# RG-LRU's second half in RWKV's buffers, and RWKV's sample steps in LRU's stream

## The chip, the core and the metric

The kernel runs on one core of a Trainium2 chip. The metric is the device time of one execution in microseconds; before the change it was 1579.41 us, the median of three runs (1573.84 to 1581.77). One further execution was taken with the profiler; it took 1583.56 us, and the trace quoted here is of that one.

## The reference, cut to what matters

One layer of a hybrid recurrent decoder, for a prompt of 1024 tokens from a zero state and for 8 sample sequences of one token each that continue from given states. The normalised input of width 1024 goes through one projection of 3456 columns, whose output feeds three groups of heads side by side:

```
pr, ph, pl = split(xn @ w_in)                       # RWKV, HGRN, LRU columns
# A) RWKV-7, 6 heads of 64, token by token
S = S * w_t + (S @ -kk_t) outer (kk_t * a_t) + v_t outer k_t ;  out_t = S @ r_t
o_r = (groupnorm(out) + sum(r * k * r_k) * v) * g
# B) HGRN2, 6 heads of 64
S = f_t * S + (1 - f_t) outer i_t ;  o_t = S^T q_t ;  o_h = rmsnorm(o) * g_norm * silu(gate)
# C) RG-LRU, 256 channels
xc = conv4(xb) ;  r = sigmoid(xc @ wa + ba) ;  i = sigmoid(xc @ wx + bx)
h_t = a_t * h_{t-1} + sqrt(1 - a_t^2) * i_t * xc_t ;  o_l = h * gelu(gate)
x = x + concat(o_r, o_h, o_l) @ w_out
x = x + relu(rmsnorm(x) @ w1)^2 @ w2 ;  y = rmsnorm(x)
```

The new states of all three groups are outputs as well. For the 8 sample sequences the recurrences are one step each.

## The kernel before, in words

**The phases.** All data is float32. A weight column of 128 is split into a high part `wh` and a low part `wl`, the activations into `xh` and `xl`, and each dense product is three matmuls per row tile of 128 (`wh` with `xh`, `wh` with `xl`, `wl` with `xh`; `dense_steps`). The mixed phase (the first half of the span) makes the input projections column by column (`in<column>_<half>_<start>`, 48 matmuls a column in the second half, in two chunks of 256 and 264 tokens), and beside them runs the recurrences, whose matmuls are small. Then come the output projection (`out`), the norm and the MLP (`up`, `dn`). Tokens 0 to 511 are half 0; tokens 512 to 1023 and the 8 sample tokens are half 1 (520 columns). The projections come in the order `ORDER`: in half 1 `w0 r0 h0 r1 r2 h1 h2 l0 l1`, so LRU's two tiles are last. Its `l0` is columns 2944 (`xb`) and 3200 (`gl`), `l1` is 3072 and 3328; the last HGRN column ahead of them is 2816.

**What sets the order.** The order of TensorE's instructions is written by a planner, `weave`, while the program is built. It holds seven streams (generators) and a filler, the dense work. A step of a stream ends by yielding a number, an estimate of how long the other engines need before the next step, or an event that it waits for. `weave` keeps a model clock `now`; at each turn it takes a stream that is due, and the filler if none is. The other engines' instructions are placed by the framework's scheduler, by readiness and priority. The streams are RWKV's chain (`rw_chain`), two of its inverse (`rw_inverse`), its operands (`rw_operands`), its finish (`rw_finish`), HGRN (`hgrn`), and LRU (`lru`). RWKV works in twelve parts (three pairs of heads `j`, two halves, two quarters of 256 tokens), HGRN in six (`j` and half), LRU in four (tile `t` and half). In names of tiles the numbers are `j` or `t`, then half, then quarter.

**Buffers that gate the projections.** A projected column of HGRN or LRU is kept in one of eight `hpm` buffers (520 + 3 wide) in SBUF, one of RWKV in one of six `pm` buffers (520 wide). A projection takes its buffer with `take`, which waits for the planner's count `free`. HGRN takes four (`f`, `q`, `i`, `g`) and gives them back at the end of `hg_run`, that is after the part's own sample step (`hg_sample`: `hsrow`, `hso`, `hsq`); RWKV takes three and gives them back when the operands of the second quarter are made; LRU takes two, `xb` and `gl`, and gives them back at its end. LRU's gelu scratch `lq` and its convolved input `lxc` have one buffer each, shared by the two tiles of a half. The output projection uses `pm` buffers too, without `take`: the residual `xr` (a transfer from `xt`) and the squares `sq`.

**LRU's tail.** `lru` makes the gelu of `gl` (L1156 to L1159), convolves `xb` into `lxc` (L1165 to L1170), makes two gates with block-diagonal matmuls (`lg`), a square root and a scan on the Vector engine (L1202), and multiplies by the gelu (L1206).

**RWKV's sample steps.** `rw_sample_lora` makes the three low-rank terms of the sample tokens (`s_lora`), and `rw_sample(j)` the one step of the pair `j`: `s_kk` (a norm), `rows_sa` and `rows_v` (the state's row sums, whose second operand is a diagonal product of `v`, made by GpSimd), `rso` (the output), `s_mean` and `s_var` (group norm). Each is one or two matmuls with Vector's work before and after it. They stand in HGRN's stream: `rw_sample(j)` runs before `hg_run(j, 1)`. Their state `s_st`, scratch `s_tm` and diagonal product `s_dg` take HGRN's own scratch buffers (tags `kh`, `qe`, `kt`).

**PSUM.** Five kinds of banks: `big` (2, dense products), `ra` (2, RWKV's inverse), `ch` (1, the chain), `h` (2, HGRN and the samples), and `o` (1). A user of `o` asks for it with `bank_o`, which waits in the planner's model until `L_O` = 1.6 us after the last use (`used_o`); on the chip a user waits for the reader of the use before.

**Weights.** Each column's weight comes by one transfer of SP's queue into `raw`; the Scalar engine makes `wh` and minus `wh` in `wl`, and a transfer that GpSimd issues adds the weight into `wl`. There are two buffers each of `wh` and `wl`, one of `raw`.

Of the kernel before, what the change touches and what calls it, by code (L numbers as in the profile page):

```python
# [17 lines left out]
P = 128  # L18
# [3 lines left out]
NB = 8  # L22
# [30 lines left out]
def kernel(ctx: ExitStack, tc: tile.TileContext, i, o):  # L53
# [397 lines left out]

    def shifted(hf, col, name, out, tag, bufs):

        k = col // P
        pr = rwp.tile([P, HT + 16], F32, tag="praw", name=f"praw_{name}", bufs=1)
        pm = rwp.tile([P, HW], F32, tag=tag, name=f"pm_{name}", bufs=bufs)

        def evac(pt, c0, n):
            take_out(hf, pr[:, c0:c0 + n], pt)

        yield from in_proj(hf, col, evac, shift=True)
        mu = vec("mu", k)
        n = HT if hf == 0 else HW
        G.tensor_scalar(pm[:, :n], pr[:, :n], omm[:, k:k + 1], 0.0, op0=ALU.mult, op1=ALU.add)
        V.scalar_tensor_tensor(pm[:, 1:HT], pr[:, 0:HT - 1], mu, pm[:, 1:HT], op0=ALU.mult, op1=ALU.add)
        if hf == 0:
            G.tensor_copy(bnd[:, k:k + 1], pr[:, HT - 1:HT])
        else:
            V.scalar_tensor_tensor(pm[:, 0:1], bnd[:, k:k + 1], mu, pm[:, 0:1], op0=ALU.mult, op1=ALU.add)
            V.scalar_tensor_tensor(pm[:, HT:HW], pr[:, HW:HW + NB], mu, pm[:, HT:HW], op0=ALU.mult, op1=ALU.add)  # L470
        out.append(pm)
# [320 lines left out]
    def rw_sample_lora():  # L792
        tcol = slice(HT, HW)
        xwa, sg = lora[1]
        out = hgp.tile([P, 3, 3, NB], F32, name="s_lora")
        for q, (w, x) in enumerate(((wup, xwa), (aup, xwa), (gup, sg))):
            pl = ps("h", f"s_lora{q}")
            for j in range(3):
                mm(pl[:, j * NB:(j + 1) * NB], w[:, j * P:(j + 1) * P], x[:, tcol])
            V.tensor_copy(out[:, q], pl[:, 0:24].rearrange("p (j b) -> p j b", b=NB))  # L800
        return out

    def rw_sample(j, lora):
# [11 lines left out]
        st = hgp.tile(B3, F32, tag="kh", name=f"s_st{j}", bufs=1)  # L815
        tm = hgp.tile(B3, F32, tag="qe", name=f"s_tm{j}", bufs=1)
        dg = hgp.tile(B3, F32, tag="kt", name=f"s_dg{j}", bufs=1)
# [11 lines left out]
        G.tensor_tensor(dg, bc(id64[:, None, :], B3), bc(v[:, :, None], B3), op=ALU.mult)  # L829
        yield D21  # L830
        pn = ps("h", f"s_kk{j}")
        mm(pn[:, 0:NB], bones, q)
        V.tensor_scalar(q, pn[:, 0:NB], 1e-24, None, op0=ALU.max)
# [11 lines left out]
        def sums(x, name):  # L845

            pd = ps("h", f"rows_{name}{j}")
            mm(pd, bones, x.rearrange("p b v -> p (b v)"))
            return pd.rearrange("p (b v) -> p b v", v=64)
# [4 lines left out]
        pd = sums(tm, "sa")  # L854
        V.tensor_tensor(tm, pd, cols(ka), op=ALU.mult)
        V.tensor_tensor(st, st, tm, op=ALU.add)
        yield D24
        pd = sums(dg, "v")
# [4 lines left out]
        po = ps("h", f"rso{j}")  # L863
        for b in range(NB):
            for h in range(2):
                hp = slice(h * 64, h * 64 + 64)
                mm(po[hp, b:b + 1], st[hp, b, :], r[hp, b:b + 1])
        V.tensor_copy(os_, po[:, 0:NB])
        yield D26
        pn = ps("h", f"s_mean{j}")  # L870
        mm(pn[:, 0:NB], bones, os_)
        V.scalar_tensor_tensor(os_, pn[:, 0:NB], -1.0 / 64.0, os_, op0=ALU.mult, op1=ALU.add)
        V.tensor_tensor(q, os_, os_, op=ALU.mult)
# [9 lines left out]
        V.tensor_tensor(mix[j][:, T:TS], os_, g, op=ALU.mult)  # L883

# [244 lines left out]
    def lru_proj(t, hf):  # L1129
# [3 lines left out]
        for w in ("xb", "gl"):  # L1133
            yield from take("hpm")
            x.append(hp_tile(f"l{w}{t}_{hf}"))
        xb, gl = x
# [7 lines left out]
    def lru(t, hf):  # L1144
        yield ("lru", t, hf)
        xb, gl = lruin[t, hf]
        gq = hgp.tile([P, HW], F32, tag="lq", name=f"lq{t}_{hf}", bufs=1)
# [59 lines left out]
        free["hpm"] += 2  # L1207
# [17 lines left out]
    def mixed(k, hf):  # L1225

        if k < 3:
            return [("P", 6 * hf + 2 * k + 1)] + [("HG", k, 1)] * hf
        return [("HG", k - 3, hf) if k < 6 else ("LRU", k - 6, hf)]

    def out_proj(hf):
# [12 lines left out]
        def evac(m, c0, cn, pt, xt):  # L1244
# [3 lines left out]
            if m == 0:  # L1248
                act(a, xm, AF.Square)
            else:  # L1250
                sq = rwp.tile([P, HW], F32, tag="pm", name=f"sq{m}_{c0}", bufs=RPM)
                act(sq[:, :cn], xm, AF.Square)
                V.tensor_tensor(a, a, sq[:, :cn], op=ALU.add)
# [3 lines left out]
        def load(m):  # L1257
            ws[m] = next_w(m + 1 < lead or m >= lead)
            xts[m] = rwp.tile([P, HW], F32, tag="pm", name=f"xr{m}_{hf}", bufs=RPM)
# [99 lines left out]
    def hgrn():  # L1359
# [3 lines left out]
        for hf in range(2):  # L1363
            if hf == 1:
                yield ("lora", 1)
                s_lora = rw_sample_lora()
            for j in range(3):
                if hf == 1:
                    yield from rw_sample(j, s_lora)
                yield from hg_run(j, hf)  # L1370

# [56 lines left out]
    def norms():  # L1428
        yield from norm2(*CH[0], lambda nm: rwp.tile([P, HW], F32, tag="pm", name=nm, bufs=RPM))
# [3 lines left out]
    with tc.manual_schedule(engines={mybir.EngineType.PE}):  # L1433
# [3 lines left out]
               each(lru, *((t, hf) for hf in range(2) for t in range(2)))], dense_work)  # L1437
# [166 lines left out]
```

## Time and profile before

| | |
|---|---|
| time, median of three runs | 1579.41 us (1573.84 to 1581.77) |
| profiled execution | 1583.56 us |
| its span | 1581.8 us |
| granted TensorE clock, mean | 0.972 |
| TensorE matmul busy | 1500.9 us, 95% of the span |
| TensorE weight load | 84% |
| Vector, Scalar, GpSimd | 48%, 42%, 24% |

The profile names the engines PE (TensorE matmul), PEld (its weight load, which overlaps), DVE (Vector), ACT (Scalar), POOL (GpSimd) and SP (which issues transfers). The span is the time from the first to the last instruction in the trace. The clock row of the page gives, for 40 equal slices of 39.5 us, the clock that TensorE was granted, in tenths (9 is 90% or more). A row of the timeline has start, duration in us, engine, line, operation and tiles (out<-in), shapes, a count, and in brackets the idle time ahead of it with what ended it. A row of the waits has the waiting engine's instruction, what released it, total us, times and the longest.

### The profile page before, as it was taken

What the parts mean: (1) busy time and instruction counts of PE and PEld (TensorE: products, weight loads), DVE (VectorE), ACT (ScalarE), POOL (GpSimd) and SP (SyncE); (2) the same over time, 40 slices, a digit from 0 to 9 for tenths busy, and PEclk for the clock granted to TensorE, in tenths of its full rate; (3) what the DMA queues carried; (4) which work ended last, traced back from release to release, by engine and by line L of the source; (5) the groups of instructions that cost most, each with busy time, mean ns of one, the idle gap of its engine ahead of it and who ended that gap; (6) DMA issues with size and microseconds to landing.
All of it is one profiled execution on the core that took longest, in us unless ns stands there. A gap on an engine that the chain in (4) does not pass through costs nothing.

```text
span 1581.8 us, 31488 instructions
## 1 busy us (share of the span) xinstructions
PE 1500.9 (95%) x13112; PEld 1322.7 (84%) x13112; DVE 757.3 (48%) x1799; ACT 665.3 (42%) x1433; POOL 382.5 (24%) x531
## 2 busy tenths in 40 slices
PE   8989999999998899978999999999999999999997
PEld 6767777888898888866798899889898989988887
DVE  7777866756566665574555222222222222222224
ACT  4544656546544556255434324232332323233232
POOL 4553323224335324323312110101111010101011
PEclk9989999998999999799999999999999999999999
DMA  4334334344434334235442544535344454544242
GB/s 152 125 68 96 84 81 94 79 83 98 91 75 96 74 81 91 62 73 124 119 128 81 107 80 99 102 83 104 83 104 83 102 92 85 102 86 101 47 93 108
DMA packets 53086, 146.98 MB, mean 93 GB/s; under 512 B 6960, under 2 KB 7248, under 8 KB 52944
## 3 DMA queue, kind: packets, MB, share of 16 engines
q0 software_dynamic: 22976, 65.33, 24.9%
q1 hardware_dynamic: 29824, 79.61, 16.1%
q8 instruction: 103, 1.69, 0.5%
q14 instruction: 39, 0.32, 0.1%
q10 hardware_dynamic: 144, 0.04, 0.0%
HBM read 138.87 MB, written 6.07 MB: 92 GB/s over the span
## 4 chain that ended last, share of the span: by engine, by line
PE 72%; DVE 10%; issue 6%; ACT 5%; DMA 4%; POOL 2%; POOLq 0%; SPq 0%; DVEq 0%; ACTq 0%
PE up L76 22%; PE dn L76 19%; PE in L76 13%; PE out L76 4%; PE ch L76 2%; PE W L76 2%; PE Y L76 2%; PE sc L76 1%; PE gram L76 1%; DMA wl_out<-in_w_out 1%; DVE rq L1035 1%; PE ho L76 1%; DMA raw_in<-in_w_in 1%; DMA wl_w<-in_w 1%; ACT gsq L768 1%
## 5 line engine op out<-in xcount | busy, mean ns | idle before, releaser
L76 PE MATMUL in<-xl,wh_in 128*128 128x512 f32 (+3 forms) x648 | 223.4, 345 | 2.1 <-DVE xl L385 2.1
L76 PE MATMUL in<-xh,wh_in 128*128 128x512 f32 (+3 forms) x648 | 223.9, 345 | 0.0
L76 PE MATMUL dn<-hh,wl_w 128*128 128x264 f32 (+2 forms) x696 | 223.2, 321 | 0.3 <-DMA wl_w<-in_w 0.2
L76 PE MATMUL dn<-hh,wh_w 128*128 128x264 f32 (+2 forms) x696 | 222.8, 320 | 0.0
L76 PE MATMUL dn<-hl,wh_w 128*128 128x264 f32 (+2 forms) x696 | 222.7, 320 | 0.0
L76 PE MATMUL in<-xh,wl_in 128*128 128x512 f32 (+3 forms) x648 | 221.4, 342 | 0.5 <-DVE wl_in L293 0.3
L1492 DVE TENSOR_TENSOR mix<-mix,dn 128x512 f32<-128x512 f32 (+2 forms) x192 | 98.4, 512 | 243.4 <-PE dn L76 243.4
L296 POOL DMA_DIRECT2D wl_w<-in_w x86 | 75.2, 877 | 575.4 <-ACT hh L1422 305.9
L291 ACT ACTIVATE wh_w<-raw_w 128x512 fp32r<-128x512 f32 (+1 forms) x90 | 70.7, 785 | 281.6 <-PE dn L76 228.0
L1421 DVE SCALAR_TENSOR_TENSOR rl<-up,rl 128x512 f32<-128x512 f32 (+2 forms) x96 | 49.5, 516 | 204.5 <-ACT rl L1420 204.4
L76 PE MATMUL up<-nxh,wh_w 128*128 128x264 f32 (+1 forms) x512 | 145.9, 285 | 0.1
L76 PE MATMUL up<-nxl,wh_w 128*128 128x264 f32 (+1 forms) x512 | 145.0, 283 | 0.5 <-POOL nxl L1318 0.5
L76 PE MATMUL up<-nxh,wl_w 128*128 128x264 f32 (+1 forms) x512 | 145.3, 284 | 0.0
L76 PEld LDWEIGHTS dn<-hh,wl_w 128*128 128x128 f32 x696 | 130.8, 188 | 14.1 <-DMA wl_w<-in_w 4.4
L76 PEld LDWEIGHTS dn<-hl,wh_w 128*128 128x128 f32 x696 | 130.9, 188 | 10.1
L76 PEld LDWEIGHTS dn<-hh,wh_w 128*128 128x128 f32 x696 | 131.0, 188 | 9.3
L76 PEld LDWEIGHTS in<-xl,wh_in 128*128 128x128 f32 x648 | 127.4, 197 | 13.4 <-DVE xl L385 4.2
L76 PEld LDWEIGHTS in<-xh,wl_in 128*128 128x128 f32 x648 | 127.1, 196 | 11.1 <-issue 1.0
L76 PEld LDWEIGHTS in<-xh,wh_in 128*128 128x128 f32 x648 | 127.3, 196 | 10.6 <-issue 0.7
L1420 ACT ACTIVATE rl<-up 128x512 f32<-128x512 f32 (+2 forms) x96 | 43.3, 451 | 141.0 <-PE up L76 140.9
L76 PE MATMUL up<-nl,wh_w 128*128 128x512 f32 x256 | 101.5, 397 | 0.0
L76 PE MATMUL up<-nh,wl_w 128*128 128x512 f32 x256 | 101.5, 396 | 0.0
(461 smaller groups left out, 3328.3 us busy)
## 6 DMA issues: line engine op xcount, KB each, us to landing
raw_in<-in_w_in SPq DMA_DIRECT2D x53, 512.0 KB, 3.4
wl_in<-in_w_in POOLq DMA_DIRECT2D x43, 512.0 KB, 5.7
raw_w<-in_w SPq DMA_DIRECT2D x32, 512.0 KB, 3.5
raw_w<-in_w SPq DMA_DIRECT2D x64, 256.0 KB, 2.7
wl_w<-in_w POOLq DMA_DIRECT2D x58, 256.0 KB, 4.1
wl_w<-in_w POOLq DMA_DIRECT2D x28, 512.0 KB, 5.6
raw_out<-in_w_out SPq DMA_DIRECT2D x16, 512.0 KB, 3.5
out_y_prompt<-yt SPq DMA_DIRECT2D x16, 256.0 KB, 2.0
```

The costliest lines, as they stand in the source:

```text
L76: PE.matmul(out, lhsT, rhs, start=start, stop=stop)
L291: act(wh[:, ks], raw[:, ks], AF.Copy)
L296: G.dma_start(wl[:, ks], src[:, ks], accum_op=ALU.add)
L768: act(sq, raw[:, g * 64:(g + 1) * 64], AF.Square, bias=sums[:, 0, g:g + 1], accum_out=sums[:, 1, g:g + 1])
L1035: V.tensor_tensor(qp[g][hp, h, :], qef[hp, gc], q[hp, gc], op=ALU.mult)
L1420: act(rl[:, :n], pt[:, :n], AF.Relu)
L1421: V.scalar_tensor_tensor(rl[:, :n], pt[:, :n], 0.0, rl[:, :n], op0=ALU.max, op1=ALU.mult)
L1492: V.tensor_tensor(x2[m][:, c0:c0 + n], x2[m][:, c0:c0 + n], pt[:, :n], op=ALU.add)
```

## The change

Three things are edited.

1. LRU's projections and its gelu scratch. `lru_proj` takes three buffers (`xb`, `gl`, `gq`) instead of two: in half 0 three `hpm`, in half 1 three `pm`. The scratch `gq` was the shared `lq` buffer. All `pm` buffers become 523 wide instead of 520 (`pm_tile`). `lru` gives three back.
2. RWKV's sample steps move from HGRN's stream to LRU's: after LRU's half 0 come the low-rank terms, the three sample steps, and then LRU's half 1. The output projection waits for an event of each sample step (`RS`) instead of the end of HGRN's part.
3. The sample steps' buffers. Their matmuls write the one bank `o` through `bank_o` instead of the two banks `h`. The state `s_st` takes LRU's `xc` buffer, the scratch `s_tm` the `lq` buffer that LRU has left. The diagonal product has no buffer of its own any more: it is written into `s_tm` after the state update that reads it.

```diff
+    def pm_tile(name):
+        return rwp.tile([P, HW + 3], F32, tag="pm", name=name, bufs=RPM)
...
     def rw_sample_lora():
...
-            pl = ps("h", f"s_lora{q}")
+            pl = yield from bank_o(f"s_lora{q}")
             for j in range(3):
                 mm(pl[:, j * NB:(j + 1) * NB], w[:, j * P:(j + 1) * P], x[:, tcol])
+            used_o()
...
     def rw_sample(j, lora):
...
-        st = hgp.tile(B3, F32, tag="kh", name=f"s_st{j}", bufs=1)
-        tm = hgp.tile(B3, F32, tag="qe", name=f"s_tm{j}", bufs=1)
-        dg = hgp.tile(B3, F32, tag="kt", name=f"s_dg{j}", bufs=1)
+        st = hgp.tile([P, HW], F32, tag="xc", name=f"s_st{j}", bufs=1)[:, 0:NB * 64].rearrange("p (b v) -> p b v", v=64)
+        tm = hgp.tile(B3, F32, tag="lq", name=f"s_tm{j}", bufs=1)
...
-        G.tensor_tensor(dg, bc(id64[:, None, :], B3), bc(v[:, :, None], B3), op=ALU.mult)
         yield D21
-        pn = ps("h", f"s_kk{j}")
+        pn = yield from bank_o(f"s_kk{j}")
         mm(pn[:, 0:NB], bones, q)
+        used_o()
...
         V.tensor_tensor(st, st, tm, op=ALU.add)
+        G.tensor_tensor(tm, bc(id64[:, None, :], B3), bc(v[:, :, None], B3), op=ALU.mult)
         yield D24
-        pd = sums(dg, "v")
+        pd = yield from sums(tm, "v")
...
-        pn = ps("h", f"s_var{j}")
+        pn = yield from bank_o(f"s_var{j}")
         mm(pn[:, 0:NB], bones, q)
         mm(pn[:, NB:2 * NB], bones, bo)
+        used_o(5.0)
...
+        ev(("RS", j), 1.5)
...
     def lru_proj(t, hf):
...
-        for w in ("xb", "gl"):
-            yield from take("hpm")
-            x.append(hp_tile(f"l{w}{t}_{hf}"))
-        xb, gl = x
+        for w in ("xb", "gl", "gq"):
+            yield from take("pm" if hf else "hpm")
+            x.append((pm_tile if hf else hp_tile)(f"l{w}{t}_{hf}"))
+        xb, gl, gq = x
...
     def lru(t, hf):
...
-        xb, gl = lruin[t, hf]
-        gq = hgp.tile([P, HW], F32, tag="lq", name=f"lq{t}_{hf}", bufs=1)
+        xb, gl, gq = lruin[t, hf]
...
-        free["hpm"] += 2
+        free["pm" if hf else "hpm"] += 3
...
     def mixed(k, hf):
         if k < 3:
-            return [("P", 6 * hf + 2 * k + 1)] + [("HG", k, 1)] * hf
+            return [("P", 6 * hf + 2 * k + 1)] + [("RS", k)] * hf
...
     def hgrn():
...
         for hf in range(2):
-            if hf == 1:
-                yield ("lora", 1)
-                s_lora = rw_sample_lora()
             for j in range(3):
-                if hf == 1:
-                    yield from rw_sample(j, s_lora)
                 yield from hg_run(j, hf)
+
+    def lru_and_samples():
+        for t in range(2):
+            yield from lru(t, 0)
+        yield ("lora", 1)
+        s_lora = yield from rw_sample_lora()
+        for j in range(3):
+            yield from rw_sample(j, s_lora)
+        for t in range(2):
+            yield from lru(t, 1)
...
-               each(lru, *((t, hf) for hf in range(2) for t in range(2)))], dense_work)
+               lru_and_samples()], dense_work)
```

The order of TensorE is the same in both programs up to the place where `s_lora` now stands, and again from the second half's output projection on. Between these the planner writes another order; three places follow. The rows are line, operation, tiles (out<-in, with a serial number at each name's end), shape, and a count.

**TensorE where column 2944 begins (the first column of LRU's half 1).** Before, between the last product of column 2816 and the first of 2944, with the rest of that stretch left out at the dots (`W`, `Y` are RWKV's inverse, `ch` its chain, `oT` and `gate` its finish; `ho`, `hoT` HGRN's output, `hsrow`, `hso`, `hsq` HGRN's sample step of part 1):

```order
L76 MATMUL in2816_1_256_7845<-xh7_3302,wl_in2816_1_7577 128x264
...
L76 MATMUL W3_2_1_1_8067<-xm_2_1_1_7737,sa_2_1_1_7735 64x64 x8
L81 MATMUL hoT_1_1_8096<-ident_79,hot_1_1_8012 128x128 x4
L76 MATMUL Y3_2_1_1_8102<-ym_2_1_1_7736,wm3_2_1_1_8066 64x64 x8
...
L76 MATMUL hsrow1_8139<-hsdg1_8122,bones_84 128x512
...
L81 MATMUL oT_1_1_1_8157<-ident_79,ot_1_1_1_8077 128x128 x4
...
L76 MATMUL gate_1_1_1_8170<-pm_xg1_3608,gup_162 128x256
L76 MATMUL hso1_8173<-hq1_1_6529,hsst1_8120 64x1 x16
L76 MATMUL W5_2_1_1_8194<-xm_2_1_1_7737,sa_2_1_1_7735 32x32 x8
L76 MATMUL hsq1_8205<-hssq1_8191,bones_84 128x8
L76 MATMUL in2944_1_0_8242<-xh0_3295,wh_in2944_1_7797 128x256
```

And after the change:

```order
L76 MATMUL in2816_1_256_8007<-xh7_3302,wl_in2816_1_7650 128x264
L76 MATMUL in2944_1_0_8077<-xh0_3295,wh_in2944_1_7829 128x256
...
L76 MATMUL Y1_2_1_1_8082<-ym_2_1_1_7893,wm1_2_1_1_8028 64x64 x8
L76 MATMUL ch_1_1_1_7635<-st2_1_1_1_8021,az_186 128x64
L76 MATMUL in2944_1_0_8077<-xl1_3304,wh_in2944_1_7829 128x256
...
L76 MATMUL in2944_1_0_8077<-xh7_3302,wh_in2944_1_7829 128x256
L76 MATMUL W2_2_1_1_8123<-xm_2_1_1_7894,sa_2_1_1_7892 64x64 x8
...
L76 MATMUL hsrow1_8142<-hsdg1_8096,bones_84 128x512
L76 MATMUL ch_1_1_1_7635<-mv_1_1_1_6737,bt_1_1_1_6492 128x64
```

Column 2944 now follows 2816 at once, and the work that stood between them stands inside it and behind it.

**Vector in LRU's half 1, from the scan of tile 0 on.** Before (L1202 is tile 0's scan, L1206 its last product; L1156 to L1159 are the gelu of tile 1, L1165 to L1170 its convolution, which tile 1's gate matmul reads):

```order
L1202 SCALAR_TENSOR_TENSOR lxc0_1_8460<-lxb0_1_8232,lcar_202,lq0_1_8454 128x512
...
L1206 SCALAR_TENSOR_TENSOR mix6_75<-lgl0_1_8233,lxc0_1_8460 128x520
...
L1156 TENSOR_SCALAR lq1_1_8844<-lq1_1_8844 128x520
L1165 TENSOR_SCALAR lxc1_1_8850<-lxb1_1_8428,vt_77 128x520
L1157 TENSOR_TENSOR lq1_1_8844<-lq1_1_8844,lgl1_1_8429 128x520
L1168 SCALAR_TENSOR_TENSOR lxc1_1_8850<-lxb1_1_8428,vt_77,lxc1_1_8850 128x512
...
L1159 SCALAR_TENSOR_TENSOR lgl1_1_8429<-lq1_1_8844,lgl1_1_8429 128x520
```

After (the lines are shifted by nine: L1211 is the scan, L1215 the last product, L1165 to L1168 the gelu, L1174 to L1179 the convolution; L1069 are the state updates of HGRN's part 2):

```order
L1165 TENSOR_SCALAR lgq1_1_8506<-lgq1_1_8506 128x520
L1166 TENSOR_TENSOR lgq1_1_8506<-lgq1_1_8506,lgl1_1_8505 128x520
...
L1211 SCALAR_TENSOR_TENSOR lxc0_1_8539<-lxb0_1_8066,lcar_202,lgq0_1_8068 128x512
...
L1168 SCALAR_TENSOR_TENSOR lgl1_1_8505<-lgq1_1_8506,lgl1_1_8505 128x520
...
L1069 SCALAR_TENSOR_TENSOR hst0_2_1_9009<-hst7_2_0_4183,wl_2_1_8910,ad_2_1_9006 128x64
L1215 SCALAR_TENSOR_TENSOR mix6_75<-lgl0_1_8067,lxc0_1_8539 128x520
...
L1174 TENSOR_SCALAR lxc1_1_8886<-lxb1_1_8504,vt_77 128x520
...
L1177 SCALAR_TENSOR_TENSOR lxc1_1_8886<-lxb1_1_8504,vt_77,lxc1_1_8886 128x512
```

The gelu of tile 1 now stands around the scan of tile 0 instead of behind its end, and state updates of HGRN's part 2 stand ahead of the convolution and among its steps.

**TensorE's users of bank `o` around the sample step of pair 1.** After the change, with everything that uses other banks left out at the dots (`pw` to `bt` are the operands of RWKV's part of pair 1, half 1, first quarter):

```order
L76 MATMUL pw_1_1_0_5714<-pm_wa1_3338,wup_158 128x256
...
L76 MATMUL s_kk1_5797<-s_q1_5729,bones_84 128x8
...
L76 MATMUL pc_kk1_1_0_5826<-bones_84,t2_1_1_0_5710 128x2 x2
...
L76 MATMUL rows_sa1_5872<-s_tm1_5719,bones_84 128x512
...
L81 MATMUL pb_kk1_1_0_5898<-ident_79,t4_1_1_0_5712 128x128 x2
...
L76 MATMUL pa_1_1_0_5949<-pm_wa1_3338,aup_159 128x256
...
L76 MATMUL rows_v1_5969<-s_tm1_5719,bones_84 128x512
...
L81 MATMUL vT_1_1_0_6010<-ident_79,bt_1_1_0_5983 128x128 x4
...
L76 MATMUL rso1_6065<-sm_r_176,s_st1_5718 64x1 x16
...
L76 MATMUL s_mean1_6103<-s_os1_5733,bones_84 128x8
...
L76 MATMUL s_var1_6141<-s_q1_5729,bones_84 128x8
...
L81 MATMUL bt_1_1_0_6228<-ident_79,kz_185 128x128 x4
```

Before, these operands stood together, the sample step came behind them, and it wrote the `h` banks:

```order
L76 MATMUL pw_1_1_0_5717<-pm_wa1_3338,wup_158 128x256
...
L76 MATMUL pc_kk1_1_0_5740<-bones_84,t2_1_1_0_5713 128x2 x2
...
L81 MATMUL pb_kk1_1_0_5822<-ident_79,t4_1_1_0_5715 128x128 x2
...
L76 MATMUL pa_1_1_0_5873<-pm_wa1_3338,aup_159 128x256
...
L81 MATMUL vT_1_1_0_5931<-ident_79,bt_1_1_0_5924 128x128 x4
...
L76 MATMUL bonus_1_1_0_6104<-t2_1_1_0_5713,bones_84 128x256
...
L76 MATMUL s_kk1_6235<-s_q1_6197,bones_84 128x8
...
L76 MATMUL rows_sa1_6325<-s_tm1_6186,bones_84 128x512
...
L76 MATMUL s_var1_6501<-s_q1_6197,bones_84 128x8
```

The six uses of the sample step now alternate with those of the operands in the one bank.

More of the change, by code (lines that the diff above doesn't have):

```diff
@@ L455, in shifted @@
         pr = rwp.tile([P, HT + 16], F32, tag="praw", name=f"praw_{name}", bufs=1)
-        pm = rwp.tile([P, HW], F32, tag=tag, name=f"pm_{name}", bufs=bufs)
+        pm = pm_tile(f"pm_{name}") if tag == "pm" else rwp.tile([P, HW], F32, tag=tag, name=f"pm_{name}", bufs=bufs)
         def evac(pt, c0, n):
@@ L845, in sums @@
         def sums(x, name):
-            pd = ps("h", f"rows_{name}{j}")
+            pd = yield from bank_o(f"rows_{name}{j}")
             mm(pd, bones, x.rearrange("p b v -> p (b v)"))
+            used_o()
             return pd.rearrange("p (b v) -> p b v", v=64)
@@ L853, in rw_sample @@
         yield D23
-        pd = sums(tm, "sa")
+        pd = yield from sums(tm, "sa")
         V.tensor_tensor(tm, pd, cols(ka), op=ALU.mult)
         V.tensor_tensor(st, st, tm, op=ALU.add)
+        G.tensor_tensor(tm, bc(id64[:, None, :], B3), bc(v[:, :, None], B3), op=ALU.mult)
         yield D24
-        pd = sums(dg, "v")
+        pd = yield from sums(tm, "v")
         V.tensor_tensor(tm, pd, cols(kn), op=ALU.mult)
@@ L862, in rw_sample @@
         yield D25
-        po = ps("h", f"rso{j}")
+        po = yield from bank_o(f"rso{j}")
         for b in range(NB):
@@ L867, in rw_sample @@
                 mm(po[hp, b:b + 1], st[hp, b, :], r[hp, b:b + 1])
+        used_o()
         V.tensor_copy(os_, po[:, 0:NB])
         yield D26
-        pn = ps("h", f"s_mean{j}")
+        pn = yield from bank_o(f"s_mean{j}")
         mm(pn[:, 0:NB], bones, os_)
+        used_o()
         V.scalar_tensor_tensor(os_, pn[:, 0:NB], -1.0 / 64.0, os_, op0=ALU.mult, op1=ALU.add)
@@ L1250, in evac @@
             else:
-                sq = rwp.tile([P, HW], F32, tag="pm", name=f"sq{m}_{c0}", bufs=RPM)
+                sq = pm_tile(f"sq{m}_{c0}")
                 act(sq[:, :cn], xm, AF.Square)
@@ L1258, in load @@
             ws[m] = next_w(m + 1 < lead or m >= lead)
-            xts[m] = rwp.tile([P, HW], F32, tag="pm", name=f"xr{m}_{hf}", bufs=RPM)
+            xts[m] = pm_tile(f"xr{m}_{hf}")
             nc.gpsimd.dma_start(xts[m][:, :n], i["xt"][m * P:(m + 1) * P, s0:s0 + n])
@@ L1428, in norms @@
     def norms():
-        yield from norm2(*CH[0], lambda nm: rwp.tile([P, HW], F32, tag="pm", name=nm, bufs=RPM))
+        yield from norm2(*CH[0], pm_tile)
         for c in CH[1:]:
```

## The prediction

> **What bounds the kernel now.** I read the page first (part 1, then the slices), then busy time by stage, then TensorE's row-by-row timeline where a stage loses time, and last the list of who waited for whom.
>
> ```profile
> span 1581.8 us, 31488 instructions
> PE 1500.9 (95%) x13112; PEld 1322.7 (84%) x13112; DVE 757.3 (48%) x1799; ACT 665.3 (42%) x1433; POOL 382.5 (24%) x531
> PEclk9989999998999999799999999999999999999999
> ```
>
> TensorE is busy 95% of the span, so time can come only from its idle stretches and from the stretches at a low clock. The lowest slice of the clock row (a 7) lies about 633 to 672 us, inside the second half of the mixed phase, which the change rearranges. Busy time in five stretches around it (columns: stretch, its length, busy us and count of PE, PEld, DVE, ACT, POOL, granted clock, DMA share, GB/s):
>
> ```profile
> 580.00:621.60 41.60, 40.41 (x669) 37.09 (x668) 25.11 (x69) 25.68 (x64) 13.51 (x21) 1.00 0.36 78
> 621.60:632.17 10.57, 7.46 (x176) 6.57 (x172) 5.58 (x19) 7.71 (x40) 6.22 (x9) 1.00 0.59 135
> 632.17:643.20 11.03, 9.77 (x94) 7.53 (x95) 5.13 (x16) 0.65 (x3) 4.65 (x7) 0.50 0.06 25
> 643.20:652.65 9.45, 9.45 (x57) 9.16 (x58) 4.23 (x15) 0.61 (x2) 4.67 (x5) 0.50 0.10 29
> 652.65:662.00 9.35, 9.08 (x65) 7.92 (x65) 6.22 (x17) 2.66 (x4) 1.70 (x4) 1.00 0.49 103
> ```
>
> Up to 621.6 PE is nearly full at clock 1.00. Then 3.1 us idle, then 20.5 us at clock 0.50. The timeline of PE there:
>
> ```profile
> 602.71 0.43 PE L76 MATMUL ch<-st,az 128*128 128x64 f32 x2
> 603.15 0.28 PE L76 MATMUL in<-xh,wl_in 128*128 128x256 f32 x1
> 603.27 0.28 PE L76 MATMUL in<-xh,wh_in 128*128 128x264 f32 x1
> ...
> 629.54 0.63 PE L81 MATMUL hoT<-ident,hot 128*128 128x128 f32 x4 [1.65 <-DVE gs L765]
> 630.10 0.68 PE L76 MATMUL Y<-ym,wm 64*64 64x64 f32 x16
> 632.58 1.12 PE L76 MATMUL W<-xm,sa 64*64 64x64 f32 x16 [1.43 <-DVE rh L724]
> 633.63 2.07 PE L76 MATMUL hsrow<-hsdg,bones 128*128 128x512 f32 x2
> 639.28 1.19 PE L76 MATMUL gate<-pm_xg,gup 128*128 128x256 f32 x2 [0.84 <-DVE mix L782]
> 643.58 0.41 PE L76 MATMUL in<-xl,wh_in 128*128 128x256 f32 x1
> 643.80 0.41 PE L76 MATMUL in<-xh,wl_in 128*128 128x256 f32 x1
> ```
>
> Dense products (`in`) follow each other every 0.12 us at 603; between 621.6 and 643.2 there is none, only the small matmuls of the recurrences, each waiting for another engine; after it they come every 0.22 us. I call this the hole. Its cause stands in the code, not in a row: LRU's half-1 projections take two `hpm` slots, all eight are held by HGRN's parts 1 and 2 of that half, and part 1 gives its four back only after its sample step (`hsq` of part 1 is the last matmul before `in` resumes).
>
> Who waited for whom on PE from 340 to 830 us (total, times, longest):
>
> ```profile
> PE lg L76 <- DVE lxc L1168: 6.0, 1, 6.0
> PE out L76 <- DMA wl_out<-in_w_out: 3.1, 2, 2.0
> PE gate L76 <- DVE mix L782: 2.5, 3, 1.0
> PE pb_kk L81 <- DVE s_bo L839: 2.3, 1, 2.3
> PE ho L76 <- DVE hst L1060: 1.8, 3, 0.9
> PE s_var L76 <- DVE s_q L873: 1.4, 1, 1.4
> PE ho L76 <- ACT ad L1051: 1.1, 1, 1.1
> PE bonus L76 <- ACT kt L544: 0.4, 1, 0.4
> ```
>
> Apart from the hole, the largest wait is LRU's last gate matmul, 6.0 us at 711.
>
> **The change, part by part.** *(a) LRU half 1 in RWKV's slots.* The projections of LRU's second half now take `pm` slots, which RWKV's operands release before HGRN's part 1 ends. In the new PE order the dense work of column 2944 begins right behind column 2816, and `hsrow`, `hso`, `hsq` of part 1 stand inside it. What was in the hole is still done, beside dense work. Idle time recovered: (10.57 - 7.46) + (11.03 - 9.77) = 4.4 us. The clock: 9.77 + 9.45 = 19.2 us were busy at 0.50. Two shapes tell what full clock gives. One is the dense spacing, 0.22 against 0.12 (45% less). The other is `W`, 1.12 at half clock, of which the timeline has just ahead, still at 1.00:
>
> ```profile
> 627.22 0.68 PE L76 MATMUL W<-xm,sa 64*64 64x64 f32 x14
> ```
>
> That is 0.68 for 14 of its 16 (39% less). I take 40%: 7.7 us. Together 12.1 us. Bounds: 4.4 (the clock falls elsewhere instead) to 4.4 + 9.6 = 14.0 (everything at half clock scales by two). I stay near the upper end because both shapes were measured and the small work gets dense neighbours.
>
> The Trainium skill ("TensorE: Matmul & The Clock Gate", Terms) prices a throttled stretch at its length times one minus the clock share: 20.5 x 0.5 = 10.2 us, an estimate, which would make the sum below 2.5 us better. The same page (Part 1) has the full clock return after about 3.4 us of sustained work; the row 643.20:652.65 shows 9.45 us of gapless matmuls still at 0.50, so the trace agrees on the half clock and not on how soon it ends.
>
> *(b) The tail of LRU.* `gq`, the gelu scratch, no longer shares one buffer between LRU's tiles 0 and 1. Vector's rows ahead of the 6.0 us wait:
>
> ```profile
> 706.57 0.42 DVE L1156 TENSOR_SCALAR lq<-lq 128x520 f32<-128x520 f32 x1
> 707.36 0.69 DVE L1157 TENSOR_TENSOR lq<-lq,lgl 128x520 f32<-128x520 f32 x1
> 709.67 0.69 DVE L1159 SCALAR_TENSOR_TENSOR lgl<-lq,lgl 128x520 f32<-128x520 f32 x1
> 735.06 1.57 DVE L1060 SCALAR_TENSOR_TENSOR hst<-hst,wl,ad 128x64 f32<-128x64 f32 x5
> ```
>
> The first two move into tile 0's square-root wait: -1.1. The state updates `hst` of HGRN part 2 move ahead of that gate matmul, six of them at 1.57 / 5: +1.9, and in return `ho`, now behind the gate matmul, finds them done: -1.8 - 1.1. The buffer `xc` is still shared, so the 6.0 us wait itself stays. Sum -2.1; bounds -4.0 (no `hst` cost) to +6.0 (the same wait once more).
>
> *(c) Samples on bank `o`.* 21 uses (3 for the lora, 6 for each of three samples) leave the two `h` banks for the single `o` bank, where each use must wait for the reader of the one before. For RWKV's own uses of `o` the waits for a reader are `gate` 2.5 and `bonus` 0.4, 2.9 us on some 70 uses (10 in each of six half-1 parts, 8 of LRU, a few left from half 0): 0.04 each. 21 x 0.04 = +0.9. Bounds: 0 to 21 x 1.0 = +21 (the longest one each time); I take the mean, since the kernel's planner spaces these uses as it does the others.
>
> *(d) Samples earlier.* They keep their instructions: per sample the state load, the store, and the same Vector, Scalar and GpSimd operations; the diagonal product moves into `tm` behind the state update. Their waits (`pb_kk` behind `s_bo` 2.3, `s_var` 1.4) are rearranged, not removed: 0, bounds -3.7 (both vanish) to +3.7 (both twice). Behind a waiting `s_var` on PE stand RWKV's chain and the dense products.
>
> *(e) The queues.* The transfers that are moved past (count, KB, us to landing), GpSimd's issues of such adds (x86: 75.2 us, 877 ns each), and, for (f), the two casts that make a weight's buffers:
>
> ```profile
> xr<-in_xt POOLq DMA_DIRECT2D x8, 256.0 KB, 3.8
> wl_in<-in_w_in POOLq DMA_DIRECT2D x23, 512.0 KB, 5.7
> L296 POOL DMA_DIRECT2D wl_w<-in_w x86 | 75.2, 877 | 575.4 <-ACT hh L1422 305.9
> 712.91 1.06 ACT L291 ACTIVATE wh_out<-raw_out 128x1024 fp32r<-128x1024 f32 x1
> 714.00 1.06 ACT L295 ACTIVATE wl_out<-wh_out 128x1024 fp32r<-128x1024 f32 x1
> ```
>
> The two loads of `xr` now stand later on POOL, since their slots are LRU's: `xr0` takes a free slot, `xr1` waits for LRU tile 0's scan. Behind `xr1` stand the chain's `ws` and then the weight adds of `out3`; the `ws` needs a state that PE produces next to the gate matmul that waits for the same tile 0. So 0; bounds 0 to +3.8, one `xr` landing. SP's order of weight loads does not move against the dense products.
>
> *(f) Weights.* Without the hole a buffer freed by one column must be refilled while the next is multiplied: 2 x 1.06 + 0.88 + 5.7 = 8.7 us. The thinnest column is 3072 (48 products at 0.12, one `Y` 0.68, three `ch` 0.43, one `gram` of 32 small matmuls taken as a `Y`: 8.4): +0.3, bounds 0 to +2.
>
> Sum: -12.1 - 2.1 + 0.9 + 0 + 0 + 0.3 = -13.0 us. The profiled execution took 1583.6 us (span 1581.8, 1.8 around it), so 1570.6 for it; it is 4.2 above the median of the runs, 1579.4. On the median: 1566.4, and I say 1567.
>
> **The rivals.** *The clock goes elsewhere.* The new order has two stretches almost without dense work: state product, chain end, `W` and `gram` of column 128, and `hS`, `sc`, `ho`, `Y` in column 2816. If each loses the clock as the hole did, (a) keeps only its idle part: -13.0 + 7.7 = -5.3, 1574. For it: the trace's hole. Against it stands a like stretch of the same half:
>
> ```profile
> 414.00:421.60 7.60, 7.00 (x127) 6.50 (x125) 3.31 (x11) 5.53 (x24) 1.62 (x3) 1.00 0.64 139
> ```
>
> It kept its clock, so the waits inside the hole matter, not the small matmuls alone.
>
> *The hole stays*, with another keeper: 2944's weights or its `pm` slots come late. For it: only POOL's order, where these weights stand behind the chain's `ws`. Against it: the columns before are filled with small work. Time 1579.
>
> *More than the hole*: both sample waits (3.7) and half of the gate wait (3) go as well: -13.0 - 6.7, 1560.
>
> *Slower: bank `o` becomes the serial resource.* Vector is the reader of most sample uses; when it is late, PE stands at the next `o` matmul and everything behind it waits. The gain of 13.9 without (c) is gone at 0.66 us a use; half a per cent slower than before (7.9 us; about what a measurement here can tell from no change) needs 1.04 us each, 1587. For it: `gate` has waited 1.0. Against it: three such waits in the whole half. The Trainium skill ("PSUM — Partial Sum Buffer", Engine vs sequencer instructions) says that matmuls start and complete in program order; by that rule one late reader would hold all of PE, and the 6.0 us at 711, with dense products queued behind `lg`, agrees.
>
> **How the numbers follow.** Forecast 0.57, clock elsewhere 0.20, hole stays 0.07, more 0.08, slower 0.08. The forecast's own range is 1560 to 1573: (a) between 10 and 14, (b) and (d) 3 either way. The whole range must reach the clock's 1574 and the unmoved 1579, with 2 us of the runs' own scatter (1573.8 to 1581.8) above it, and 1560 with as much below, rounded: 1556 to 1581; outside lie the slower rival and tails of some 0.1. Faster by over 0.5% is below 1571.5: most of the forecast (0.52), all of "more" and a fifth of the clock's case, 0.64. Slower by over 0.5%: 0.08. Within: 0.28.
>
> **What would show it.** Right: a clock row without the 7, column 2944 following 2816 with no stretch of 5 us free of `in`, `ho` of HGRN part 2 without a wait, the gate matmul of LRU tile 1 still waiting 4 to 8 us. Wrong: a new slice at clock 0.7 or 0.8 before 700 us; many waits of PE for readers of bank `o` (`s_`, `rows_`, `pa`, `pb_kk`) adding up to more than 5 us; `out` waiting for `wl_out` longer than 3.1 in all.

## The result and the profile after

The changed kernel takes 1585.54 us (median; 1578.74 to 1592.09, 12 runs) against 1579.48 for the kernel before (1573.84 to 1582.99, 12 runs). The ratio is 1.0051, with a 95% interval of 1.0034 to 1.0069: slower by half a per cent, about 8 us by the ratio (6.1 by the two medians). The forecast was 1567, faster by 13.

The page of the changed kernel (span; busy times; the clock row in 40 slices):

```profile
span 1584.6 us, 31459 instructions
PE 1493.5 (94%) x13112; PEld 1318.5 (83%) x13112; DVE 761.3 (48%) x1799; ACT 665.4 (42%) x1433; POOL 382.0 (24%) x531
PEclk9989999999999998998999999999999999999999
```

The slice at 0.7 is gone and PE's busy time fell by 7.4 us, yet the span grew. To see where, I cut the rearranged part into four stretches. Before (stretch, length, then busy us and count of PE, PEld, DVE, ACT, POOL, then granted clock):

```profile
340.00:460.00 120.00, 114.88 (x1487) 107.06 (x1486) 69.35 (x213) 63.15 (x162) 41.34 (x62) 0.96 0.40 89
460.00:570.00 110.00, 101.58 (x1285) 92.11 (x1284) 68.17 (x209) 55.64 (x152) 43.09 (x61) 0.97 0.36 81
570.00:690.00 120.00, 111.84 (x1496) 100.77 (x1488) 74.25 (x206) 59.33 (x168) 40.35 (x57) 0.91 0.33 75
690.00:800.00 110.00, 92.65 (x742) 77.11 (x735) 66.25 (x138) 52.23 (x104) 34.42 (x42) 0.94 0.45 114
```

And after the change:

```profile
340.00:460.00 120.00, 110.01 (x1428) 101.85 (x1425) 68.33 (x200) 59.98 (x156) 38.59 (x57) 0.97 0.39 85
460.00:570.00 110.00, 100.53 (x1277) 90.77 (x1275) 73.30 (x211) 54.63 (x148) 47.55 (x67) 0.98 0.38 87
570.00:690.00 120.00, 106.92 (x1570) 98.07 (x1569) 68.96 (x203) 56.04 (x151) 35.88 (x52) 0.93 0.30 68
690.00:800.00 110.00, 93.30 (x714) 79.24 (x714) 69.53 (x147) 58.94 (x127) 35.60 (x44) 0.94 0.45 113
```

Two losses can be read from such a row: idle time (length minus PE's busy time) and what the clock takes (busy time times one minus the clock). Idle went from 39.1 to 49.2 us over the four, the clock's loss from 23.3 to 18.4. So the clock was won, 4.9 us, and idle time lost, 10.2; the sum is +5.3. It can be only a rough match for the 6 to 8 us of the runs: the two profiled executions, single ones, differ by 2.8 us in span. Half of the new idle time lies in 340 to 460 and the other half in 570 to 690.

Who PE waited for in these two stretches of the changed kernel (total, times, longest; the first three rows are from 340 to 460, the others from 570 to 690):

```profile
PE pa L76 <- DVE t L561: 3.0, 1, 3.0
PE vT L81 <- ACT t L567: 2.8, 1, 2.8
PE ch L76 <- DVE st L740: 1.6, 2, 1.0
...
PE W L76 <- DVE xm L700: 4.0, 1, 4.0
PE hsq L76 <- DVE hssq L1124: 3.2, 1, 3.2
PE ch L76 <- DVE st L740: 3.1, 2, 2.2
```

All are waits for Vector or Scalar, a few microseconds each, for RWKV's work (`pa`, `vT`, `W`, `ch`) and HGRN's (`hsq`). Some of these waits have a stretch at half clock behind them and some have none: in the 4 us behind the 2.8 us wait of `vT` at 426 the mean clock was 0.60, in the 4 us behind the 3.0 us wait of `pa` at 387 it was 1.00. Around the 4.0 us wait of `W` at 608:

```profile
604.40:608.12 3.72, 0.02 (x1) 0.00 (x0) 2.28 (x5) 2.16 (x5) 0.10 (x1) 1.00 0.00 0
608.12:614.94 6.82, 6.54 (x78) 5.93 (x79) 1.73 (x6) 5.10 (x9) 2.66 (x3) 0.50 0.36 86
614.94:625.00 10.06, 10.06 (x144) 9.37 (x143) 3.26 (x11) 4.29 (x9) 0.67 (x3) 1.00 0.25 47
```

The clock is at 0.50 for 6.82 us behind it, which costs another 3.3.

### The profile page after: what moved, and what is told of

Same layout as the page of the kernel before. It is cut to its first block, busy times and chain, and to the rows that moved or that the text cites. A ratio compares the mean times of both kernels' runs of the same rounds, so it can differ in the third digit from the quotient of the medians.

```text
span 1584.6 us, 31459 instructions
## 1 busy us (share of the span) xinstructions
PE 1493.5 (94%) x13112; PEld 1318.5 (83%) x13112; DVE 761.3 (48%) x1799; ACT 665.4 (42%) x1433; POOL 382.0 (24%) x531
## 4 chain that ended last, share of the span: by engine, by line
PE 73%; DVE 11%; ACT 5%; DMA 5%; issue 4%; POOL 2%; POOLq 0%; ACTq 0%; DVEq 0%; SPq 0%
PE up L76 22%; PE dn L76 20%; PE in L76 13%; PE out L76 4%; PE ch L76 3%; PE W L76 2%; PE Y L76 2%; PE sc L76 1%; PE gram L76 1%; PE ho L76 1%; DMA raw_in<-in_w_in 1%; DVE rq L1044 1%; ACT gsq L771 1%; DMA wl_w<-in_w 1%; DMA raw_out<-in_w_out 1%
## 5 line engine op out<-in xcount | busy, mean ns | idle before, releaser
L76 PEld LDWEIGHTS in<-xh,wh_in 128*128 128x128 f32 x648 | 125.6, 194 | 10.2 <-issue 0.7
L76 PE MATMUL up<-nh,wh_w 128*128 128x512 f32 x256 | 101.5, 396 | 0.0
```

What stands on the lines that cost most here:

```text
L76: PE.matmul(out, lhsT, rhs, start=start, stop=stop)
```

## The experiments

Three theories were in dispute from the start: V, later C, that the sample steps run beside HGRN and the two delay each other (collision); O, the single bank `o`; and R, that the work of the hole only returns elsewhere. All kernels below were compared with the kernel before on the same chip; the changed kernel itself was not run again beside them. I give each ratio to the kernel before, and microseconds as (ratio - 1) x 1579. On that scale the changed kernel is at +8.1 (5.4 to 10.9).

**One part alone: LRU's buffers.** The change to `lru_proj`, `lru` and `pm_tile`, and nothing else:

```diff
-        for w in ("xb", "gl"):
-            yield from take("hpm")
+        for w in ("xb", "gl", "gq"):
+            yield from take("pm" if hf else "hpm")
...
```

> Only LRU's part of the change (three pm buffers in half 1, the gelu scratch with them); the sample steps stay in HGRN's stream, on the h banks, with HGRN's scratch. Theory V (Vector's order: the loss comes from the sample steps running beside HGRN, so that RWKV's short Vector steps queue behind HGRN's long ones): the hole's 14 us come back nearly whole, 9 to 13 us faster than before, about 1568. Theory O (the one bank o): the same, 9 to 13 faster, since no sample step is on bank o. Theory R (the hole's work only returns elsewhere: the dense work brought forward is lost again at LRU's tail, where the gate matmul waits for Vector): within 3 us of before, with the wait of lg at 8 us or more.

Ratio 0.9946 (0.9923 to 0.9969): 8.5 us faster, 1569.83 in the median, just under the 9 to 13 that V and O gave. The hole's stretches in this kernel:

```profile
621.60:632.17 10.57, 9.15 (x198) 8.34 (x198) 5.23 (x17) 6.85 (x34) 4.93 (x7) 1.00 0.56 136
632.17:643.20 11.03, 11.03 (x118) 9.89 (x116) 7.43 (x22) 4.63 (x14) 5.17 (x6) 1.00 0.28 65
643.20:660.00 16.80, 16.13 (x135) 14.79 (x135) 7.94 (x26) 4.60 (x9) 8.73 (x12) 0.70 0.37 91
```

The two stretches of the hole are full at clock 1.00, but a later one falls to 0.70 and takes 4.8 us back. Theory R falls for this part: the work does not merely return later, and `lg` waits 5.1 us, not 8.

**The other part alone: the samples.** The changed kernel with LRU's projections and gelu scratch as before.

```diff
-        for w in ("xb", "gl", "gq"):
-            yield from take("pm" if hf else "hpm")
+        for w in ("xb", "gl"):
+            yield from take("hpm")
...
```

> Only the samples' part of the change (LRU's stream, bank o, tags xc and lq); LRU's projections and scratch stay as before, so the hole in front of column 2944 stays, shorter by the sample step that HGRN's stream no longer has. Theories V and O: the samples' move costs some 15 us, the shorter hole gives 3 to 6 back: 8 to 14 us slower than before, about 1590. Theory R: the move costs nothing by itself: within 4 us of before.

Ratio 1.0012 (0.9985 to 1.0039): +1.9 us, no difference that the runs can tell. Theories V and O, with 8 to 14 slower, missed; the number is the one that R gave, within 4 us of before. But no theory named that +1.9 alone and -8.5 alone make +8.1 together, 14.7 more than their sum. The trace suggests two reasons. The dense work up to column 2816 lasts to 641.5 us here instead of 621.6, and HGRN's part 1 only to 651 instead of 643, so the hole had already shrunk to 11.4 us and kept its clock:

```profile
641.50:652.90 11.40, 8.80 (x175) 7.47 (x174) 5.82 (x20) 7.43 (x25) 4.38 (x7) 0.96 0.53 119
```

There was little left for LRU's buffers to win. And the gate matmul `lg` waits here for no longer than 1.0 us at a time, while in the changed kernel it waits 7.8 (row below), a wait worth 5.8 us there. The 8.5 that LRU's buffers no longer win and these 5.8 would make up the 14.7; that is an account from the rows, not a run of its own. It gives R a share: with both parts, LRU's tail does lose time.

**The bank.** The changed kernel with the 21 uses of the samples on the two `h` banks.

```diff
-        pn = yield from bank_o(f"s_kk{j}")
+        pn = ps("h", f"s_kk{j}")
...
-        used_o()
```

> The changed kernel with the 21 sample uses back on the two h banks; stream and buffers as in the changed kernel. Theory O: the waits of pa, vT and kt for readers of bank o (about 8 us in the changed kernel from 340 to 640 us) go, and most of the loss with them: 8 to 12 us faster than before, about 1570. Theory V: the waits for Vector's order stay: within 4 us of the changed kernel, 1582 to 1588. Theory R: within 3 us of the changed kernel too.

Ratio 1.0033 (1.0012 to 1.0055): +5.2 us, 2.9 below the changed kernel, with intervals that overlap. Theory O, which had this kernel 8 to 12 us faster than before, falls. TensorE's order changes with the bank as well. The waits of `pa` and `vT` are gone, and others stand in their place; from 340 to 460:

```profile
PE rows_v L76 <- POOL s_tm L858: 5.5, 1, 5.5
PE s_mean L76 <- DVE s_os L870: 1.9, 1, 1.9
```

So the waits for readers of `o` look like the place where PE met late engines, and not like their cause.

**HGRN held behind the samples.** One line more in the changed kernel:

```diff
             for j in range(3):
+                if hf == 1:
+                    yield ("RS", j)
                 yield from hg_run(j, hf)
```

> The changed kernel with one line more: part j of HGRN in half 1 waits for the planner's event of sample step j, so that HGRN does not start earlier than the samples, as before the change; samples still in LRU's stream and on bank o. Theory V: the waits of W, ch and hoT for Vector (about 15 us from 340 to 700 us in the changed kernel) fall by half: 6 to 12 us faster than the changed kernel, about 1576. Theory O: bank o is as full as in the changed kernel, within 4 us of it. Theory R: within 4 us of it.

Ratio 0.9926 (0.9903 to 0.9949): 11.7 us faster than before and 19.7 faster than the changed kernel, at 1567.3 in the median. That is more than the 6 to 12 of theory V; the waits of `W`, `ch` and `hoT` for Vector from 340 to 700 us fell by half, as V had it, from 17.4 to 8.7. It uses bank `o` as the changed kernel does. Its four stretches (the profiled execution, at 1574.7, is the longest of its ten runs):

```profile
340.00:460.00 120.00, 113.02 (x1459) 105.27 (x1460) 70.48 (x207) 62.81 (x161) 41.48 (x62) 0.99 0.42 93
460.00:570.00 110.00, 103.74 (x1330) 93.00 (x1330) 72.75 (x224) 55.05 (x150) 46.17 (x66) 0.97 0.31 73
570.00:690.00 120.00, 112.90 (x1630) 103.31 (x1625) 75.25 (x207) 64.40 (x177) 37.54 (x53) 0.94 0.34 78
690.00:800.00 110.00, 93.47 (x670) 80.51 (x670) 64.46 (x136) 49.81 (x99) 34.44 (x43) 0.94 0.46 122
```

Idle time is 36.9 us in all instead of 49.2, and the clock takes 16.6 instead of 18.4: 14.1 us less, of which 5.2 from 340 to 460. In TensorE's order the one large difference is that HGRN's part 0 of half 1 starts behind sample step 0 instead of beside it; what follows shifts with it.

**No sample steps.** The changed kernel with the body of `rw_sample` cut to the load and the store of the state, and `s_lora` left out (e9); the second (e10) with HGRN's part 0 held back besides:

```diff
             for j in range(3):
+                if (j, hf) == (0, 1):
+                    yield ("hg", 0, 1)
+                    yield 25.0
                 yield from hg_run(j, hf)
```

> The changed kernel without the computation of RWKV's sample steps (their state is loaded and stored unchanged; the low-rank terms are left out too); HGRN starts as in the changed kernel, with nothing beside it. Theory C (collision: the sample steps and HGRN's part 0 delay each other): 20 to 25 us faster than the changed kernel, about 1562, of which some 6 are the steps' own work. Theory H (HGRN's part 0 is simply too early for the dense work that must cover it, samples or not): only 5 to 9 us faster than the changed kernel, about 1578.

> As e9, without the sample steps' computation, and HGRN's part 0 of half 1 held for 25 us of the planner's clock, to where it starts in the version that waits for the samples. Theory C: within 4 us of e9. Theory H: 8 to 14 us faster than e9.

Ratios 0.9873 (0.9846 to 0.9899) and 0.9880 (0.9854 to 0.9906): -20.1 and -18.9 us, the same. Without the steps it does not matter when HGRN's part 0 starts, so theory H falls. Four kernels now stand in a square: with the steps +8.1, and -11.7 with HGRN held; without them -20.1, and -18.9 held. So the steps cost 28 us in the changed kernel and 7 with HGRN held behind them. The difference, about 21 us (7 either way, an estimate that takes the four intervals as independent), is what the steps and HGRN's earlier start cost only together.

**The same, the other way round.** The sample steps wait for the end of HGRN's part 0:

```diff
         s_lora = yield from rw_sample_lora()
+        yield ("HG", 0, 1)
         for j in range(3):
```

> The changed kernel with one line more: the sample steps wait for the end of HGRN's part 0 of half 1, instead of HGRN for the steps. Step 0 then runs alone between HGRN's parts 0 and 1, steps 1 and 2 run beside part 1. Theory C (any sample step beside HGRN's work costs): one of the two overlaps is gone, and the later one is longer: 2 to 6 us faster than the changed kernel. Theory S (what counts is the stage at 600 us, where HGRN's part 1 and RWKV's last inverse meet): that stage gets a sample step more, so no gain, or up to 6 us slower than the changed kernel.

Ratio 1.0013 (0.9992 to 1.0034): 6 us faster than the changed kernel, at the upper end of theory C's range, with intervals that just touch, and no faster than before. Steps 1 and 2 now run beside part 1.

How far does "beside" explain the times? The traces give the start of the first and the last matmul of each step and of HGRN's parts 0 and 1 of half 1 (us):

| kernel | step 0 | step 1 | step 2 | part 0 | part 1 | against before |
|---|---|---|---|---|---|---|
| before | 376-398 | 498-520 | 647-668 | 418-494 | 572-643 | 0 |
| changed | 374-433 | 467-496 | 529-589 | 410-490 | 567-655 | +8.1 |
| samples on `h` | 376-406 | 471-498 | 526-545 | 425-508 | 591-667 | +5.2 |
| HGRN held | 374-428 | 458-498 | 534-582 | 431-504 | 571-649 | -11.7 |
| steps behind part 0 | 493-562 | 576-617 | 622-650 | 412-487 | 557-643 | +2.1 |

In the held version step 1 still runs wholly beside part 0, and step 2 reaches into part 1; by their matmuls, only the end of step 0 no longer meets the start of part 0. With the samples on `h`, steps 0 and 2 meet no part at all, and most of the loss is still there. So running beside HGRN does not set the time by itself. That the steps and the earlier part 0 cost some 20 us together is measured; which meeting costs, and how much of it comes only from the shift of what follows, is not shown.

**Which work of the steps.** TensorE's order is that of the changed kernel in all three; the wide elementwise operations (128x512) of the steps are cut to one of eight sequences: on both engines (e11), on Vector alone (e17), on GpSimd alone (e18):

```diff
-        tm = hgp.tile(B3, F32, tag="lq", name=f"s_tm{j}", bufs=1)
+        tm = s_tm0
...
-        V.tensor_tensor(tm, st, cols(kk), op=ALU.mult)
-        G.tensor_tensor(st, st, cols(w), op=ALU.mult)
+        st1, tm1 = st[:, 0:1], tm[:, 0:1]
+        V.tensor_tensor(tm1, st1, cols(kk), op=ALU.mult)
+        G.tensor_tensor(st1, st1, cols(w), op=ALU.mult)
...
```

The scratch `s_tm` also gets a buffer of its own (`s_tm0`) in all three, instead of LRU's `lq`; by the run on Vector alone, both together are worth about 1 us.

> The changed kernel with TensorE's order unchanged, but the wide elementwise operations of the sample steps (four of Vector's and two of GpSimd's per step, 128x512) done for one of the eight sample sequences only; the others' states and sums are left as they are. Theory V (Vector's time: the steps' wide operations hold up RWKV's short ones): some 7 us of Vector's time go, and with them waits and half-clock stretches: 8 to 14 us faster than the changed kernel, about 1574. Theory L (the order and the latencies of the many small operations decide, not their width): within 4 us of the changed kernel.

> As e11 (TensorE's order unchanged), but only Vector's four wide operations of each sample step are cut to one of eight sequences; GpSimd's two stay whole. Theory V (Vector's time in its queue is what the others wait for): most of e11's gain, 7 to 11 us faster than the changed kernel. Theory P (GpSimd's wide operations are the cost, by the time for which they hold up short Vector operations such as the 128x8 one of 2.9 us at 472): less than 4 us faster.

> As e11 (TensorE's order unchanged), but only GpSimd's two wide operations of each sample step are cut to one of eight sequences; Vector's four stay whole. Theory V: less than 4 us faster than the changed kernel. Theory P: 6 us or more faster, and no 128x8 operation of Vector over 1 us.

Both: 0.9981 (0.9964 to 0.9997), 11 us below the changed kernel. Vector alone: 1.0045 (1.0022 to 1.0067), 1 us below, not to be told from nothing. GpSimd alone: 1.0018 (0.9998 to 1.0037), 5 us below, its interval just touching that of the changed kernel. So about 11 of the 28 us that the steps cost in the changed kernel hang on the width of these operations with PE's order unchanged, and the two single cuts do not add up to them. Theory V in its narrow form (Vector's time, 7 to 11 us) falls. P is favoured without being settled: its 6 us were not quite reached, and the intervals of the two single cuts overlap. How the rest splits between the steps' own work, the order of the many small operations and the shift of later parts stays open.

**The gate's wait.** In the changed kernel, and in the version held behind the samples, tile 1's convolved input gets a buffer of its own:

```diff
-        xc = hgp.tile([P, HW], F32, tag="xc", name=f"lxc{t}_{hf}", bufs=1)
+        if (t, hf) == (1, 1):
+            yield from take("hpm")
+            xc = hp_tile("lxc1_1")[:, 0:HW]
+        else:
+            xc = hgp.tile([P, HW], F32, tag="xc", name=f"lxc{t}_{hf}", bufs=1)
```

> The changed kernel, with the convolved input of LRU's tile 1 (half 1) in a free hpm buffer instead of the xc buffer that it shares with tile 0. Theory G (the gate matmul's wait of 7.8 us at 717 is a loss of its own, set by the shared buffer): the wait falls below 2 us, and the time by 4 to 7 us against the changed kernel, to about 1580. Rival E (the end of the mixed phase is set by Vector's and the weights' order, so that the wait goes to the next in line, out for wl_out or ho for hst): within 2 us of the changed kernel.

> The version in which part j of HGRN waits for sample step j, with the same own buffer for tile 1's convolved input. There the gate matmul waited 4.7 us. Theory G: 3 to 5 us faster than that version, about 1563. Rival E: within 2 us of it, about 1567.

In the changed kernel: 1.0014 (0.9998 to 1.0030), 5.8 us faster than it, as theory G had it, though the wait fell only to 2.6 us and not below 2. The gate's row from 690 to 800 us in the changed kernel, and then with the own buffer, where it waits for the reader of the bank's use before:

```profile
PE lg L76 <- DVE lxc L1179: 7.8, 1, 7.8
```

```profile
PE lg L76 <- DVE mix L785: 2.6, 1, 2.6
```

In the held version: 0.9932 (0.9906 to 0.9957) against 0.9926 without, no gain, though its wait of 4.7 went as well (0.7 left): there rival E holds. The kernels with all their work that beat both are the held one, with or without this buffer, and the one with LRU's part alone; their intervals overlap.

**One placement in Vector's queue.** The wait of `W` at 608 stands behind HGRN's part 2 on Vector (start, us, operation, idle time ahead):

```profile
605.84 1.27 DVE L968 TENSOR_TENSOR_SCAN b<-rmask,lf 128x256 f32<-128x256 f32 x2 [2.01 <-ACT lf L943]
607.03 0.27 DVE L696 COPY_PREDICATED ym<-cmask,Y 128x128 f32<-128x128 int32 x1
607.21 0.69 DVE L983 TENSOR_TENSOR kq<-b 128x512 f32<-128x512 f32 x1
607.81 0.44 DVE L700 STREAM_TRANSPOSE xm<-ym 128x256 f32<-128x256 f32 x1
```

The scan of a part whose first matmul is 50 us away is placed early because its input is there; it waits 2.0 us for the Scalar engine, and RWKV's `ym` and `xm` wait behind it. The edit gives `lf` a buffer that part 1 holds to its end:

```diff
-        lf = hgp.tile([P, HW], F32, tag="kq", name=f"lf{j}_{hf}", bufs=2)[:, 0:HT]
+        if (j, hf) == (2, 1):
+            lf = hgp.tile([P, NCK, C], F32, tag="qe", name=f"lf{j}_{hf}", bufs=1).rearrange("p c t -> p (c t)")
+        else:
+            lf = hgp.tile([P, HW], F32, tag="kq", name=f"lf{j}_{hf}", bufs=2)[:, 0:HT]
```

> The changed kernel with TensorE's order unchanged; the first buffer of HGRN's part 2 (lf) is taken from the tag qe, which part 1 holds to its end, so that part 2's first Vector steps (lf and the scan b) cannot stand in Vector's queue ahead of RWKV's xm at 605 us, where the scan waited 2.0 us for the Scalar engine's logarithm and TensorE 4.0 us for xm. Theory Q (in-order queues: that one placement costs the 4.0 us wait and about 3.4 us of half clock): 4 to 7 us faster than the changed kernel, about 1580, with no wait over 1 us of W for xm there. Rival N (TensorE would only wait for the next thing, and part 2's later start costs it elsewhere): within 2 us of the changed kernel.

Ratio 1.0031 (1.0010 to 1.0053): 3 us less than the changed kernel, between Q and N, but the intervals overlap. The wait itself is gone; from 570 to 690 the largest are now

```profile
PE ch L76 <- DVE st L740: 4.4, 2, 2.2
PE hsq L76 <- DVE hssq L1127: 2.7, 1, 2.7
```

That one placement is at most a small part of the loss.

## Why the prediction was wrong, by its steps

*(d), samples earlier: 0, bounds -3.7 to +3.7.* This is the step that failed. It counted the steps' instructions and the two waits that they had, and said that these are rearranged. It did not ask what the steps would now run beside, and it put the term at nothing. In HGRN's stream a sample step and HGRN's part took turns; in LRU's stream nothing keeps them apart, and the planner's clock, which counts only TensorE's time and fixed delays, sees no conflict on Vector and GpSimd. Measured: (c) and (d) together, +0.9 in the sum, cost 16.6 us on top of LRU's buffers (from -8.5 to +8.1), and -3.2, no cost, when HGRN is held behind the steps (from -8.5 to -11.7), on the same bank and with the same instructions of the steps. Through which wait the 20 us between the two arrangements come stays open; the width of the steps' operations on Vector and GpSimd accounts for some 11 of the 28 us that the steps cost.

*(a), LRU's half 1 in RWKV's slots: -12.1, and (b), (f) beside it, -13.9 together.* Alone, the mechanism was right: it measures -8.5 (-12.2 to -4.9). The clock's part was taken too high, since 4.8 us of clock loss came back right behind; and one of its two shapes is weaker than it says, since 0.68 us for 14 matmuls are 0.78 for 16, 31% below 1.12 and not 39%. Beside the moved samples the gain is gone: from +1.9 to +8.1 the buffers cost 6 us. The sign for it came only in part: the 7 of the clock row is gone, but TensorE still had stretches of 5.6 and 5.8 us without `in`, at 643 and 651, and half clock from 652 to 659.

*(b), the tail.* `ho` of part 2 waits no longer in the changed kernel, as said. The gate's wait was forecast to stay at 6.0 and grew to 7.8. It is worth 5.8 us in the changed kernel and nothing in the held one.

*(c), bank `o`: +0.9.* No cost clear of the noise shows: the held version is on bank `o`, and the `h` banks gave 2.9 us with overlapping intervals. The sign that I had named for a wrong forecast did appear: `pa`, `vT`, `kt`, `pb_kk` and `rows_sa` waited 8.5 us from 340 to 640. Read as a price it would have led to the wrong rival.

*(e), (f), queues and weights.* `out` waits 4.2 us for `wl_out` from 690 to 800 instead of 3.1, and `in` 1.2 for `wl_in` in 570 to 690: small, above the +0.3.

*The rivals.* "Clock elsewhere" came true in part (the slice from 594 to 634 us is at 0.8, as is the one from 713 to 753), but the clock as a whole was won and idle time decided. The result lies on the slower side, for a mechanism that no rival named; that the bank's rival gave 1587, close to the measured 1585.5, is luck. The sum treated the two parts of the change as independent: alone they are -8.5 and +1.9, and neither tells +8.1.

## What to carry to other kernels

When work is moved from one stream to another, ask first what kept it apart from its old neighbours: a serial stream also keeps its members from meeting on the engines that they share, and a planner that models one engine's time may not replace that. One added wait (`yield ("RS", j)`) turned +8 into -12 us here. Test two-part changes in their parts: an edit that closes a stall is worth little once another edit has shrunk the same stall.

## What the runs showed of the hardware

A Vector operation of 128x8, which takes 0.23 and 0.25 us in the other two sample steps, lasted 2.91 us in the changed kernel, and ended as three GpSimd operations without a pause between them ended (start, us):

```profile
472.35 2.91 DVE L840 TENSOR_SCALAR s_q<-s_a,vt 128x8 f32<-128x8 f32 x1
```

```profile
471.89 1.33 POOL L152 TENSOR_TENSOR ir_kk<-ir_kk,mhalf 128x4 f32<-128x4 f32 x1
473.20 1.03 POOL L1108 TENSOR_TENSOR hsst<-hsst,hfs 128x512 f32<-128x512 f32 x1
474.20 1.03 POOL L856 TENSOR_TENSOR s_st<-s_st,s_w 128x512 f32<-128x512 f32 x1
```

With GpSimd's operations thinned it took 0.22 at the same place. Of the profiles with this order of TensorE, that of the version with another buffer for `lf` shows it too (2.90 us), the others do not, so it seems to be a matter of alignment; it fits the 5 us that GpSimd's width was worth without proving them. The Trainium skill ("SBUF — State Buffer", Who interferes with whom) says that Vector and GpSimd share a pair of ports, that whoever comes first holds it for its whole instruction, and that `tensor_scalar` can need it. The trace agrees in that the Vector operation is drawn out and GpSimd's operations keep their 1.03 us; here it lasts past the end of one GpSimd instruction and through the two behind it.
